# A hybrid decoder layer on one core: position mixes a block earlier, their gelu product on VectorE, and a scan without its empty state

## The chip, the cores and the metric

One core of one Trainium2 chip runs the whole layer in one launch. The metric is device time in microseconds (us). The time before is the median of three runs.

## What is computed

One decoder layer on 1024 tokens of 1024 channels, float32. A normalised input is projected to all inputs of three token mixers; their outputs, each projected and weighted by a sigmoid gate, are summed, projected and added to the residual; a squared-ReLU MLP follows.

```python
def gmlp_mixer(za, ln_g, ln_b, w_s, b_s):              # mixer A
    u, v = jnp.split(jax.nn.gelu(za), 2, axis=-1)
    v = layer_norm(v, ln_g, ln_b)
    vc = v.reshape(bsz, nc, GMLP_CHUNK, GMLP_GROUPS, GMLP_GROUP_DIM)
    w = jnp.where(causal, w_s, 0)                      # 8 groups, 128x128 lower triangle
    mixed = jnp.einsum('gts,bcsgd->bctgd', w, vc) + b_s.T[:, :, None]
    return u * mixed.reshape(bsz, seq, GMLP_WIDTH)

def ssd_mixer(...):                                    # mixer C, 8 chunks of 128 tokens
    ...
    y_diag = jnp.einsum('bgcls,bgrcls,bcsgrp->bclgrp', cb, decay, xdt)
    states = jnp.einsum('bcsgn,bgrcs,bcsgrp->cbgrpn', bc, decay_states, xdt)
    def step(h, inp):
        dec, st = inp
        return h * dec[..., None, None] + st, h        # the state ahead of each chunk
    _, prev = lax.scan(step, jnp.zeros_like(states[0]), (chunk_decay, states))
    y_off = jnp.einsum('bclgn,cbgrpn,bgrcl->bclgrp', cc, prev, jnp.exp(a_cs))
    y = y_diag + y_off + x32 * d_skip
    ...

hn = rms_norm(h, norm_mix_g);  proj = hn @ w_in        # split into za, zb, zc, xbc, dt, gates
merged = sum(sigmoid(gate_k) * (mixer_k @ w_branch_k)) # A gMLP, B recurrence (RG-LRU), C scan (SSD)
h = h + merged @ w_out
h = h + relu(rms_norm(h) @ w_mlp_up)**2 @ w_mlp_down;  out = rms_norm(h)
```

The state ahead of chunk 0 is zero, and the state behind the last chunk (7) is used by nothing.

## The kernel before, in words

Activations lie with channels on the 128 partitions and tokens along the free side. A large float32 product is made from a high part (rounded to float32r) and a low part, three matmuls for each 128x128 weight tile: high by high, high by low, low by high. `split` (L128) makes such a pair: a copy on ScalarE (L132) and a subtraction on VectorE (L133).

The kernel runs in stages:

- Up to about 120 us the normalised input X is built and the V half of gMLP is projected, normalised and written to memory (`vn_d`).
- Then come 34 *units*. A unit (`one_unit`, L567) is a block of 128 output columns of `w_in`: 48 matmuls of 512 columns into a PSUM tile `ps` of two banks (pool `mainps`, two tiles), then its `post` and then `step`, which advances each pending generator by one stage. The units are four groups of the scan (B, C, two X blocks) with two heads of the recurrence each, and then eight U blocks of gMLP (`gmlp_unit`). Weights are loaded and split up to two units ahead (`ahead`); the low part is made by an accumulating DMA on GpSimd's queue (L537).
- Then come the gate blocks in pairs (class `Pair`): each pair is a scheme of seven half-size products (`p1` to `p7`, 12 matmuls each, `seventh`), with sums of weights (`Weights`: `cast1`, `sums1`, `sums2`, `cast12`, `cast34`, `cast22`) and sums of X (`x_forms`: T1 to T4, made for two pairs of k tiles in turn, four stages each). Its PSUM pool `gps` takes the four banks of `mainps` over; pool `aux` has four banks of its own.
- Branch projections, output projection and MLP follow. The change doesn't touch them.

Up to the end of the units the order on each engine is set by the framework's planner: from simulated times it takes, on each engine, the ready instruction that comes first in the program, and a tile is given a buffer when one is free. Generators (`later`, `step`) thus set the program's order, not the exact place. From the gate pairs on (`manual_schedule`) the order is the program's own. Most tiles of 128x1024 share one pool of 15 buffers (tag `act`, names `a`); tiles half as large share 16 (`half`, names `h`).

gMLP before: `post` of U block g makes the gelu of U (`gelu2`, L233 to L238: two steps on ScalarE, two on VectorE), asks for the V group g + 1 (`v_group`, L833) and puts off `stages`. These run one block later: 16 mix matmuls (L847), scale and bias on VectorE (L848), the product with the gelu on GpSimd (L850), and the store (L851). The sums of X and the first pair's weights are put off from the first step of `stages` of blocks 0 and 5.

The scan before: for each of four groups and two halves of the tokens, `rows_in` and `s1_` load decay rows (L666, L672), transpose X and B (L678, L685), weight X (L681, L682) and build the masked matrix; `s2_` makes the states of four chunks (L712) and advances the state (L723, four steps of 64 columns for each chunk); `s3_` adds the state's part (`yo`, L732), the part within the chunk (`yi`, L736) and the skip (L738 to L740), and stores.

Of the kernel before, what the change touches and what calls it, by code (L numbers as in the profile page):

```python
# [36 lines left out]
def trunk_kernel(ctx: ExitStack, tc: tile.TileContext, x, norm_mix_g, w_in, b_gate, gmlp_ln_g, gmlp_ln_b,  # L37
# [40 lines left out]
    def aux():  # L78
        return auxp.tile([P, HF], F32, tag="aux", name=nm("aux"))
# [12 lines left out]
    def hsl(h):  # L92
        return slice(h * HF, h * HF + HF)
# [451 lines left out]
    def later(gen):  # L545
        pending.append(gen)
# [106 lines left out]
    def ssd_stages(g, S):  # L653
        Bf, Cf, Xf = S["b"], S["c"], (S["x0"], S["x1"])
        hs = slice(4 * g, 4 * g + 4)
        Bt = act((P, NCH, P))
        xdt, xw, E, cb, pv, er = {}, {}, {}, {}, {}, {}

        def tok(c):
            return slice(c * P, (c + 1) * P)  # L660

        def rows_in(half):
            for q in (2 * half, 2 * half + 1):
                e = E[q] = act((P, 2, 4, P))
                for cc in range(2):
                    nc.gpsimd.dma_start(out=e[:, cc], in_=acs_v[0, 2 * q + cc, hs, :].partition_broadcast(P))  # L666

        def s1_(half):
            for j in range(2):
                t = er[half, j] = half_((P, 4, P))  # L670
                for h in range(2):
                    nc.gpsimd.dma_start(out=t[64 * h:64 * h + 64], in_=acs_v[1, half * 4:half * 4 + 4, 4 * g + 2 * j + h, :].partition_broadcast(64))  # L672
            for q in (2 * half, 2 * half + 1):
                ps = aux()
                for cc in range(2):
                    for j in range(2):
                        o = cc * 256 + j * P
                        nc.tensor.transpose(out=ps[:, o:o + P], in_=Xf[j][:, tok(2 * q + cc)], identity=ident)  # L678
                ev = ps.rearrange("p (c h d) -> p c h d", c=2, h=4)
                xdt[q], xw[q] = half_((P, 2, 4, 64)), half_((P, 2, 4, 64))  # L680
                tt(out=xdt[q], in0=ev, in1=dt[:, 2 * q:2 * q + 2, hs].unsqueeze(3).to_broadcast([P, 2, 4, 64]), op=ALU.mult)  # L681
                tt(out=xw[q], in0=ev, in1=w2[:, 2 * q:2 * q + 2, hs].unsqueeze(3).to_broadcast([P, 2, 4, 64]), op=ALU.mult)  # L682
            ps = aux()
            for i in range(4):
                nc.tensor.transpose(out=ps[:, tok(i)], in_=Bf[:, tok(half * 4 + i)], identity=ident)  # L685
            actv(Bt[:, half * 4:half * 4 + 4, :], ps.rearrange("p (c n) -> p c n", c=4), AF.Copy)
            cb[half] = aux()
            for i in range(4):
                c = half * 4 + i
                mm(cb[half][:, tok(i)], Bf[:, tok(c)], Cf[:, tok(c)], start=True, stop=True)  # L690

            cbm = half_((P, 4, P))
            tt(out=cbm, in0=cb[half].rearrange("p (c l) -> p c l", c=4), in1=tri.unsqueeze(1).to_broadcast([P, 4, P]), op=ALU.mult)
            for q in (2 * half, 2 * half + 1):
                e = E[q]
                for cc in range(2):
                    for h in range(4):
                        col = (2 * q + cc) * 16 + 4 * g + h
                        actv(e[:, cc, h, :], e[:, cc, h, :], AF.Relu, scale=-1.0, bias=acs[:, col:col + 1])
                actv(e, e, AF.Exp, scale=-1.0)  # L700
                for cc in range(2):
                    i = (2 * q + cc) % 4
                    tt(out=e[:, cc], in0=e[:, cc], in1=cbm[:, i].unsqueeze(1).to_broadcast([P, 4, P]), op=ALU.mult)

        def s2_(half):
            for q in (2 * half, 2 * half + 1):
                if q == 0:
                    pv[0] = half_((P, 2, 256))
                    nc.gpsimd.memset(pv[0][:, 0, :], 0.0)
                st = aux()  # L710
                for cc in range(2):
                    mm(st[:, cc * 256:cc * 256 + 256], Bt[:, 2 * q + cc, :], xw[q][:, cc].rearrange("p h d -> p (h d)"), start=True, stop=True)  # L712
                for cc in range(2):
                    c = 2 * q + cc
                    if c == NCH - 1:
                        continue
                    if cc == 1:
                        pv[q + 1] = half_((P, 2, 256))
                    dst = pv[(c + 1) // 2][:, (c + 1) % 2, :]
                    for h in range(4):  # L720
                        col = c * 16 + 4 * g + h
                        o = slice(h * 64, h * 64 + 64)
                        stt(out=dst[:, o], in0=pv[q][:, cc, o], scalar=etot[:, col:col + 1],  # L723
                            in1=st[:, cc * 256 + h * 64:cc * 256 + h * 64 + 64], op0=ALU.mult, op1=ALU.add)

        def s3_(half):
            tk = hsl(half)
            for j in range(2):
                yo, yi = aux(), aux()
                for i in range(4):  # L730
                    c = half * 4 + i
                    mm(yo[:, tok(i)], pv[c // 2][:, c % 2, j * P:(j + 1) * P], Cf[:, tok(c)], start=True, stop=True)  # L732
                for i in range(4):
                    c = half * 4 + i
                    for h in range(2):
                        mm(yi[64 * h:64 * h + 64, tok(i)], xdt[c // 2][:, c % 2, 2 * j + h, :], E[c // 2][:, c % 2, 2 * j + h, :], start=True, stop=True)  # L736
                y = er[half, j].rearrange("p c l -> p (c l)")
                tt(out=y, in0=yo, in1=y, op=ALU.mult)  # L738
                tt(out=y, in0=yi, in1=y, op=ALU.add)
                stt(out=y, in0=Xf[j][:, tk], scalar=dcol[:, 2 * g + j:2 * g + j + 1], in1=y, op0=ALU.mult, op1=ALU.add)  # L740
                nc.gpsimd.dma_start(out=yr_d[2 * g + j][:, tk], in_=y)

        rows_in(0)
        yield
        if g:
            yield
        s1_(0)
        yield
        s2_(0)
        yield  # L750
        s3_(0)
        rows_in(1)
        yield
        s1_(1)
        yield
        s2_(1)
        yield
        s3_(1)


    PLAIN = 6

    def lru_units(h):
        S = {}

        def post_x(ps):
# [11 lines left out]
                S["xs"].append(p_)  # L778
            if h < PLAIN:
                later(stages(False))  # L780
            elif h == 7:
                v_group(0)

        def post_g(ps):
            S["g2"] = act()
            gelu2(S["g2"], ps, T)
            later(stages(True))

        def stages(gated):
            if not gated:  # L790
# [39 lines left out]
    def v_group(g):  # L830
        if g < 8:
            v_of[g] = act((P, NCH, P))
            nc.gpsimd.dma_start(out=v_of[g], in_=vn_d[:, g * P:(g + 1) * P].rearrange("(c p) d -> p c d", p=P))  # L833

    def gmlp_unit(g):
        def stages(u2):
            if g == 0:
                later(x_forms())
            elif g == 5:
                later(first_pair())  # L840
            yield
            vg = v_of.pop(g)
            y = act()
            for half in range(2):
                ps = aux()
                for i in range(4):
                    mm(ps[:, i * P:(i + 1) * P], vg[:, half * 4 + i, :], wT[:, g, :], start=True, stop=True)  # L847
                stt(out=y[:, hsl(half)].rearrange("p (c t) -> p c t", t=P), in0=ps.rearrange("p (c t) -> p c t", t=P),  # L848
                    scalar=vh[:, LNG + g:LNG + g + 1], in1=bs[:, g, :].unsqueeze(1).to_broadcast([P, 4, P]), op0=ALU.mult, op1=ALU.add)
            nc.gpsimd.tensor_tensor(out=y, in0=y, in1=u2, op=ALU.mult)  # L850
            nc.gpsimd.dma_start(out=yd["a"][g], in_=y)  # L851

        def post(ps):
            u2 = act()
            gelu2(u2, ps, T)
            later(stages(u2))
            v_group(g + 1)

        unit_in(C_U + g * P, post)

# [51 lines left out]
    class Pair:  # L912
# [79 lines left out]
            actv(self.o[0][:, 0], self.b1, AF.Copy)  # L992

        def p2(self):
            b0 = gps.tile([P, HF], F32, tag="gps", name=nm("gps"))
            self.mul(b0, "A12", "B21", True)
            tt(out=self.o[0][:, 0], in0=b0, in1=self.o[0][:, 0], op=ALU.add)

# [916 lines left out]
```

## Time and profile before

| | |
|---|---|
| median of three runs | 1932.02 us (1931.97 to 1932.76) |
| the profiled execution, its own time | 1931.48 us |
| its span in the profile | 1929.8 us |
| TensorE busy | 1896.3 us (98%) |
| VectorE, ScalarE, GpSimd busy | 1408.0, 1010.1, 254.8 us |
| mean granted clock of TensorE | 0.997 |

The profile is of one execution. A row of the timeline has the start, the time from the first start to the last end, the engine, the line of the kernel, the operation and the tiles (out<-in), the shape and a count; behind it in brackets the engine's idle time and what ended it. Successive matmuls overlap: the distance from start to start is what one costs. TensorE (PE) and its weight load (PEld) have rows of their own; DVE is VectorE, ACT ScalarE, POOL GpSimd, SP the queue of SyncE.

### The profile page before, as it was taken

To read this page: it belongs to the slowest core of one execution; us is meant where nothing else is said; L and a number is where in the kernel's file an instruction comes from. 1 tells how busy PE (TensorE), PEld (TensorE's weight loads), DVE (VectorE), ACT (ScalarE), POOL (GpSimd) and SP (SyncE) were. 2 spreads that over 40 slices of the span, in tenths; PEclk is the share of its full clock that TensorE was granted. 3 is DMA by queue.
4 is the path that set the end of the run, shared out by engine and by line. 5 is a ranking of instruction groups with operands and counts; after the bars stand their busy time and mean duration, and the time that the engine had idled before them with its cause. 6 is when DMAs were issued, how large, how long until landed. Compare 5 with 4: busy or idle time off the path is not lost.

```text
span 1929.8 us, 23698 instructions
## 1 busy us (share of the span) xinstructions
PE 1896.3 (98%) x8928; PEld 1582.3 (82%) x8928; DVE 1408.0 (73%) x2005; ACT 1010.1 (52%) x1470; POOL 254.8 (13%) x352
## 2 busy tenths in 40 slices
PE   8999999999999999999999999999999999999998
PEld 7998888888887787878778888887888887888886
DVE  6585869787758776767767889458665567787787
ACT  6435859676634545454554544256655555253236
POOL 4112112121342000000010110000111111000000
PEclk9999999999999999999999999999999999999999
DMA  5346475565755343435298887431554458544532
GB/s 165 79 137 145 112 158 124 123 161 131 162 141 153 109 145 103 156 91 161 93 292 302 229 242 199 159 110 55 180 166 167 137 185 301 184 142 142 176 119 109
DMA packets 210439, 301.25 MB, mean 156 GB/s; under 512 B 12964, under 2 KB 125812, under 8 KB 210324
## 3 DMA queue, kind: packets, MB, share of 16 engines
q1 hardware_dynamic: 166628, 158.28, 26.5%
q0 software_dynamic: 34544, 119.69, 23.1%
q10 hardware_dynamic: 9152, 21.77, 3.2%
q8 instruction: 70, 1.15, 0.2%
q14 instruction: 45, 0.37, 0.1%
HBM read 195.75 MB, written 74.58 MB: 140 GB/s over the span
## 4 chain that ended last, share of the span: by engine, by line
PE 80%; DVE 7%; issue 6%; DMA 3%; ACT 3%; POOL 1%; POOLq 0%; DVEq 0%; ACTq 0%; SPq 0%
PE aux L487 40%; PE ps L564 16%; PE gps L487 10%; PE aux L1387 5%; PE aux L257 4%; PE aux L800 1%; DMA c<-yc_d 1%; PE aux L736 1%; DMA raw<-in_w_in_dram 1%; PE aux L732 1%; DVE wt L133 1%; PE aux L712 1%; DVE a L133 1%; ACT wt L132 1%; DMA a<-g_d 1%
## 5 line engine op out<-in xcount | busy, mean ns | idle before, releaser
L564 PE MATMUL ps<-xn,wh 128*128 128x512 f32 x1088 | 295.1, 392 | 0.0
L487 PE MATMUL aux<-b,b 128*128 128x512 f32 x1152 | 264.4, 390 | 0.7 <-DVE b L133 0.7
L487 PEld LDWEIGHTS aux<-b,b 128*128 128x128 f32 x1152 | 216.1, 188 | 46.7 <-DVE b L133 1.6
L564 PEld LDWEIGHTS ps<-xn,wh 128*128 128x128 f32 x1088 | 202.9, 188 | 42.1 <-issue 0.7
L487 PE MATMUL aux<-a,b 128*128 128x512 f32 x960 | 219.4, 389 | 0.0
L487 PEld LDWEIGHTS aux<-a,b 128*128 128x128 f32 x960 | 180.2, 188 | 37.4
L564 PE MATMUL ps<-xn,wl 128*128 128x512 f32 x544 | 168.4, 390 | 0.0
L487 PE MATMUL gps<-xn,wt 128*128 128x512 f32 x684 | 159.8, 392 | 2.1 <-DVE a L238 2.1
L487 PE MATMUL aux<-b,wt 128*128 128x512 f32 x672 | 156.9, 389 | 0.0
L487 PEld LDWEIGHTS gps<-xn,wt 128*128 128x128 f32 x684 | 128.9, 189 | 29.2 <-issue 2.5
L487 PEld LDWEIGHTS aux<-b,wt 128*128 128x128 f32 x672 | 126.2, 188 | 26.2
L132 ACT ACTIVATE b<-wt 128x1024 fp32r<-128x1024 f32 x88 | 90.7, 1052 | 85.7 <-DMA wt<-u_d 62.0
L133 DVE TENSOR_TENSOR wt<-a,wt 128x1024 fp32r<-128x1024 f32 x66 | 80.8, 1225 | 65.1 <-ACT wt L132 65.0
L564 PEld LDWEIGHTS ps<-xn,wl 128*128 128x128 f32 x544 | 102.1, 188 | 21.4
L133 DVE TENSOR_TENSOR b<-wt,b 128x1024 fp32r<-128x1024 f32 x88 | 107.2, 1219 | 15.4 <-ACT b L132 15.4
L1625 DVE TENSOR_TENSOR a<-aux,a 128x512 f32<-128x512 f32 x112 | 77.1, 688 | 49.3 <-PE aux L487 49.0
L133 DVE TENSOR_TENSOR a<-a,a 128x1024 fp32r<-128x1024 f32 (+1 forms) x68 | 66.5, 985 | 41.8 <-ACT a L132 41.7
L132 ACT ACTIVATE a<-a 128x1024 fp32r<-128x1024 f32 (+1 forms) x68 | 55.7, 833 | 53.2 <-DVE a L1577 45.4
L133 DVE TENSOR_TENSOR wt<-rt,wt 128x1024 fp32r<-128x1024 f32 x35 | 42.8, 1224 | 52.6 <-ACT wt L132 52.5
L487 PE MATMUL aux<-a,wt 128*128 128x512 f32 x336 | 78.7, 390 | 1.2 <-ACT a L1500 1.2
L132 ACT ACTIVATE wt<-a 128x1024 fp32r<-128x1024 f32 x66 | 69.6, 1055 | 12.5 <-DVE a L515 12.1
L487 PEld LDWEIGHTS aux<-a,wt 128*128 128x128 f32 x336 | 62.9, 188 | 15.0 <-ACT a L1500 2.0
(358 smaller groups left out, 3497.9 us busy)
## 6 DMA issues: line engine op xcount, KB each, us to landing
wt<-u_d SPq DMA_DIRECT2D x54, 512.0 KB
u_d<-a POOLq DMA_DIRECT2D x48, 512.0 KB, 4.9
raw<-in_w_in_dram SPq DMA_DIRECT2D x34, 512.0 KB
wl<-raw POOLq DMA_DIRECT2D x34, 512.0 KB, 5.2
g_d<-a POOLq DMA_DIRECT2D x24, 512.0 KB, 3.3
a<-g_d ACTq DMA_DIRECT2D x24, 512.0 KB
rt<-in_w_in_dram SPq DMA_DIRECT2D x19, 512.0 KB
a<-in_w_in_dram SPq DMA_DIRECT2D x19, 512.0 KB
```

The source lines that it names most:

```text
L132: actv(dst_hi, src, AF.Copy)
L133: (eng or nc.vector).tensor_tensor(out=dst_lo, in0=src, in1=dst_hi.bitcast(F32), op=ALU.subtract)
L257: mm(ps[:, :nt], X.tok(a, k, c), wk[k][w], start=(k == 0 and i == 0), stop=(k == KD - 1 and i == 2))
L487: mm(ps, lhs[l][kk], rhs[r][kk], start=(new and n == 0), stop=(n == 11), skip_group_check=not new)
L564: mm(ps[:, hsl(h)], w[wi][:, k, :], a.rhs(ai, k, h), start=(n == 0), stop=(n == 3 * KD - 1))
L712: mm(st[:, cc * 256:cc * 256 + 256], Bt[:, 2 * q + cc, :], xw[q][:, cc].rearrange("p h d -> p (h d)"), start=True, stop=True)
L732: mm(yo[:, tok(i)], pv[c // 2][:, c % 2, j * P:(j + 1) * P], Cf[:, tok(c)], start=True, stop=True)
L736: mm(yi[64 * h:64 * h + 64, tok(i)], xdt[c // 2][:, c % 2, 2 * j + h, :], E[c // 2][:, c % 2, 2 * j + h, :], start=True, stop=True)
L800: mm(ps, w[wi][:, q * P:(q + 1) * P], S["xs"][half][ai], start=(n == 0), stop=(n == 2))
L1387: mm(ps, M.tok(a, k, c), wo[nb][k][w], start=(k == 0 and a + w == 0), stop=(k == KD - 1 and a == 1))
L1625: tt(out=h, in0=ps, in1=h, op=ALU.add)
```

## The change

- **Scan.** The state product of chunk 7, the transpose of its B block and its weighted X (`xw`) are left out, and so are the two products of chunk 0 with the zero state and the rows of decay for it. The state behind chunk 0 is one copy of `st` in place of four multiply-adds with zero, and the zero fill on GpSimd goes. In `s3_`, half 0, the first two steps and the skip run on 384 columns, with a short step for chunk 0.
- **gMLP.** The mix becomes a generator of its own, `mix(g)`, put off in `post` of block g - 1 (for g = 0 in the gate unit of head 7), so that it runs one block ahead of U block g. `post` of block g then makes gelu and, on VectorE, its product with the finished mix, and stores. V groups 0 and 1 are asked for in the X units of heads 6 and 7, group g + 2 in `post` of block g.
- **Sums of X and the first pair's weights** are put off in `post` itself, one block sooner.
- **First pair.** `p2` of the first pair takes its PSUM tile from `aux`, no longer from `gps`.

```diff
@@ ssd_stages
+        def chunks_into(q):
+            return min(2, NCH - 1 - 2 * q)
...
-                    nc.gpsimd.dma_start(out=t[64 * h:64 * h + 64], in_=acs_v[1, half * 4:half * 4 + 4, 4 * g + 2 * j + h, :].partition_broadcast(64))
+                    c0 = 4 * half + (half == 0)
+                    nc.gpsimd.dma_start(out=t[64 * h:64 * h + 64, c0 - 4 * half:], in_=acs_v[1, c0:half * 4 + 4, 4 * g + 2 * j + h, :].partition_broadcast(64))
...
-                tt(out=xw[q], in0=ev, in1=w2[:, 2 * q:2 * q + 2, hs].unsqueeze(3).to_broadcast([P, 2, 4, 64]), op=ALU.mult)
+                n = chunks_into(q)
+                tt(out=xw[q][:, :n], in0=ev[:, :n], in1=w2[:, 2 * q:2 * q + n, hs].unsqueeze(3).to_broadcast([P, n, 4, 64]), op=ALU.mult)
...
-            for i in range(4):
+            nt = 4 - half
+            for i in range(nt):
                 nc.tensor.transpose(out=ps[:, tok(i)], in_=Bf[:, tok(half * 4 + i)], identity=ident)
...
-                    nc.gpsimd.memset(pv[0][:, 0, :], 0.0)
                 st = aux()
-                for cc in range(2):
+                for cc in range(chunks_into(q)):
                     mm(st[:, cc * 256:cc * 256 + 256], Bt[:, 2 * q + cc, :], ...)
...
+                    if c == 0:
+                        nc.vector.tensor_copy(out=dst, in_=st[:, :256])
+                        continue
@@ s3_
+            c0 = P * (half == 0)
...
-                for i in range(4):
+                for i in range(c0 // P, 4):
                     c = half * 4 + i
                     mm(yo[:, tok(i)], pv[c // 2][:, c % 2, j * P:(j + 1) * P], Cf[:, tok(c)], start=True, stop=True)
...
-                tt(out=y, in0=yo, in1=y, op=ALU.mult)
-                tt(out=y, in0=yi, in1=y, op=ALU.add)
-                stt(out=y, in0=Xf[j][:, tk], scalar=dcol[...], in1=y, op0=ALU.mult, op1=ALU.add)
+                tt(out=y[:, c0:], in0=yo[:, c0:], in1=y[:, c0:], op=ALU.mult)
+                tt(out=y[:, c0:], in0=yi[:, c0:], in1=y[:, c0:], op=ALU.add)
+                if c0:
+                    stt(out=y[:, :c0], in0=x_[:, :c0], scalar=d, in1=yi[:, :c0], op0=ALU.mult, op1=ALU.add)
+                stt(out=y[:, c0:], in0=x_[:, c0:], scalar=d, in1=y[:, c0:], op0=ALU.mult, op1=ALU.add)
@@ lru_units
             if h < PLAIN:
                 later(stages(False))
-            elif h == 7:
-                v_group(0)
+            else:
+                v_group(h - PLAIN)
...
             later(stages(True))
+            if h == 7:
+                later(mix(0))
@@ gmlp_unit
+    def mix(g):
+        vg = v_of.pop(g)
+        y = ya[g] = act()
+        for half in range(2):
+            ps = aux()
+            for i in range(4):
+                mm(ps[:, i * P:(i + 1) * P], vg[:, half * 4 + i, :], wT[:, g, :], start=True, stop=True)
+            stt(out=y[...], in0=ps..., scalar=vh[:, LNG + g:LNG + g + 1], in1=bs[:, g, :]..., op0=ALU.mult, op1=ALU.add)
+        yield
+
     def gmlp_unit(g):
-        def stages(u2):
-            ... (sums of X or first pair, yield, the same mix)
-            nc.gpsimd.tensor_tensor(out=y, in0=y, in1=u2, op=ALU.mult)
-            nc.gpsimd.dma_start(out=yd["a"][g], in_=y)
         def post(ps):
-            u2 = act()
+            u2, y = act(), ya.pop(g)
             gelu2(u2, ps, T)
-            later(stages(u2))
-            v_group(g + 1)
+            tt(out=y, in0=y, in1=u2, op=ALU.mult)
+            nc.gpsimd.dma_start(out=yd["a"][g], in_=y)
+            if g + 1 < 8:
+                later(mix(g + 1))
+            v_group(g + 2)
+            if g == 0:
+                later(x_forms())
+            elif g == 5:
+                later(first_pair())
@@ Pair
         def p2(self):
-            b0 = gps.tile([P, HF], F32, tag="gps", name=nm("gps"))
+            b0 = gps.tile([P, HF], F32, tag="gps", name=nm("gps")) if prev else aux()
```

More of the change, by code (lines that the diff above doesn't have):

```diff
@@ L681, in s1_ @@
                 tt(out=xdt[q], in0=ev, in1=dt[:, 2 * q:2 * q + 2, hs].unsqueeze(3).to_broadcast([P, 2, 4, 64]), op=ALU.mult)
-                tt(out=xw[q], in0=ev, in1=w2[:, 2 * q:2 * q + 2, hs].unsqueeze(3).to_broadcast([P, 2, 4, 64]), op=ALU.mult)
+                n = chunks_into(q)
+                tt(out=xw[q][:, :n], in0=ev[:, :n], in1=w2[:, 2 * q:2 * q + n, hs].unsqueeze(3).to_broadcast([P, n, 4, 64]), op=ALU.mult)
             ps = aux()
-            for i in range(4):
+            nt = 4 - half
+            for i in range(nt):
                 nc.tensor.transpose(out=ps[:, tok(i)], in_=Bf[:, tok(half * 4 + i)], identity=ident)
-            actv(Bt[:, half * 4:half * 4 + 4, :], ps.rearrange("p (c n) -> p c n", c=4), AF.Copy)
+            actv(Bt[:, half * 4:half * 4 + nt, :], ps[:, :nt * P].rearrange("p (c n) -> p c n", c=nt), AF.Copy)
             cb[half] = aux()
@@ L708, in s2_ @@
                     pv[0] = half_((P, 2, 256))
-                    nc.gpsimd.memset(pv[0][:, 0, :], 0.0)
                 st = aux()
-                for cc in range(2):
+                for cc in range(chunks_into(q)):
                     mm(st[:, cc * 256:cc * 256 + 256], Bt[:, 2 * q + cc, :], xw[q][:, cc].rearrange("p h d -> p (h d)"), start=True, stop=True)
-                for cc in range(2):
+                for cc in range(chunks_into(q)):
                     c = 2 * q + cc
-                    if c == NCH - 1:
-                        continue
                     if cc == 1:
@@ L726, in s3_ @@
         def s3_(half):
-            tk = hsl(half)
+            c0 = P * (half == 0)
             for j in range(2):
                 yo, yi = aux(), aux()
-                for i in range(4):
+                for i in range(c0 // P, 4):
                     c = half * 4 + i
@@ L736, in s3_ @@
                         mm(yi[64 * h:64 * h + 64, tok(i)], xdt[c // 2][:, c % 2, 2 * j + h, :], E[c // 2][:, c % 2, 2 * j + h, :], start=True, stop=True)
-                y = er[half, j].rearrange("p c l -> p (c l)")
-                tt(out=y, in0=yo, in1=y, op=ALU.mult)
-                tt(out=y, in0=yi, in1=y, op=ALU.add)
-                stt(out=y, in0=Xf[j][:, tk], scalar=dcol[:, 2 * g + j:2 * g + j + 1], in1=y, op0=ALU.mult, op1=ALU.add)
-                nc.gpsimd.dma_start(out=yr_d[2 * g + j][:, tk], in_=y)
+                y, x_ = er[half, j].rearrange("p c l -> p (c l)"), Xf[j][:, hsl(half)]
+                d = dcol[:, 2 * g + j:2 * g + j + 1]
+                tt(out=y[:, c0:], in0=yo[:, c0:], in1=y[:, c0:], op=ALU.mult)
[3 more added lines that the diff above has]
+                stt(out=y[:, c0:], in0=x_[:, c0:], scalar=d, in1=y[:, c0:], op0=ALU.mult, op1=ALU.add)
+                nc.gpsimd.dma_start(out=yr_d[2 * g + j][:, hsl(half)], in_=y)
         rows_in(0)
@@ L833, in v_group, with post @@
             nc.gpsimd.dma_start(out=v_of[g], in_=vn_d[:, g * P:(g + 1) * P].rearrange("(c p) d -> p c d", p=P))
-    def gmlp_unit(g):
-        def stages(u2):
+    ya = {}
+    def mix(g):
[5 more added lines that the diff above has]
+                mm(ps[:, i * P:(i + 1) * P], vg[:, half * 4 + i, :], wT[:, g, :], start=True, stop=True)
+            stt(out=y[:, hsl(half)].rearrange("p (c t) -> p c t", t=P), in0=ps.rearrange("p (c t) -> p c t", t=P),
+                scalar=vh[:, LNG + g:LNG + g + 1], in1=bs[:, g, :].unsqueeze(1).to_broadcast([P, 4, P]), op0=ALU.mult, op1=ALU.add)
+        yield
+    def gmlp_unit(g):
+        def post(ps):
+            u2, y = act(), ya.pop(g)
+            gelu2(u2, ps, T)
+            tt(out=y, in0=y, in1=u2, op=ALU.mult)
[3 more added lines that the diff above has]
+            v_group(g + 2)
             if g == 0:
@@ L840, in stages @@
                 later(first_pair())
[L841 to L850, printed above, removed]
-            nc.gpsimd.dma_start(out=yd["a"][g], in_=y)
-        def post(ps):
-            u2 = act()
-            gelu2(u2, ps, T)
-            later(stages(u2))
-            v_group(g + 1)
         unit_in(C_U + g * P, post)
```

## The prediction

> **What bounds the kernel now.** I read the page's first part, then the busy time by stretch, then TensorE's instructions in order of time around the one stretch that stood out.
>
> ```profile
> PE 1896.3 (98%) x8928; PEld 1582.3 (82%) x8928; DVE 1408.0 (73%) x2005; ACT 1010.1 (52%) x1470; POOL 254.8 (13%) x352
> ...
> 120.00:320.00 200.00, 198.84 (x997) 165.65 (x996) 153.43 (x259) 134.28 (x191) 38.92 (x61) 1.00 0.58 131
> 320.00:490.00 170.00, 169.93 (x909) 142.54 (x909) 130.93 (x204) 121.12 (x188) 38.37 (x61) 1.00 0.63 142
> 490.00:583.00 93.00, 93.00 (x500) 79.33 (x499) 62.15 (x77) 40.35 (x56) 36.26 (x26) 1.00 0.60 155
> 583.00:640.00 57.00, 52.80 (x239) 42.69 (x238) 46.47 (x50) 23.08 (x32) 13.33 (x8) 0.97 0.42 130
> ```
>
> The columns of a stretch are its length, then busy time of TensorE, its weight load, VectorE, ScalarE and GpSimd, then granted clock, DMA share and GB/s. TensorE is busy for 1896.3 of 1929.8 us. From 120 to 583 us, where the scan, the recurrence and the position mixes run, it idles 1.2 us in all: there the time is the sum of TensorE's instructions, and any instruction taken out shortens it, while work taken off VectorE or GpSimd is worth nothing by itself. The change ends at about 615 us, and the one bad place within its reach is the passage from the last U block to the first gate pair, just after 590 us:
>
> ```profile
> 590.61 3.73 PE L847 MATMUL aux<-wT,a 128*128 128x128 f32 x32
> 594.10 2.98 PE L487 MATMUL gps<-xn,wt 128*128 128x512 f32 x12
> 599.17 4.17 PE L487 MATMUL gps<-xn,wt 128*128 128x512 f32 x12 [2.10 <-DVE a L238]
> 603.14 1.06 PE L487 MATMUL aux<-h,wt 128*128 128x512 f32 x2
> 605.08 2.59 PE L487 MATMUL aux<-h,wt 128*128 128x512 f32 x10 [0.88 <-DVE wt L133]
> 607.97 3.04 PE L487 MATMUL gps<-h,wt 128*128 128x512 f32 x12 [0.30 <-ACT a L992]
> ...
> 612.37 2.56 PE L487 MATMUL aux<-xn,wt 128*128 128x512 f32 x10 [0.92 <-DVE wt L133]
> 614.77 8.32 PE L487 MATMUL gps<-xn,wt 128*128 128x512 f32 x36
> ...
> 625.65 2.88 PE L487 MATMUL aux<-h,wt 128*128 128x512 f32 x12
> 628.37 2.88 PE L487 MATMUL gps<-h,wt 128*128 128x512 f32 x12
> ```
>
> These are p1, p2, p5, p6, p3 of the first pair, 12 matmuls each. From 594.10 to 614.77 they take 20.67 us. At the steady spacing (628.37 - 625.65 = 2.72 us for 12) they need 13.60. So 7.07 us are lost here. Four waits (2.10, 0.88, 0.30, 0.92) make 4.20 of it. The clock makes another part:
>
> ```profile
> 599.17:602.00 2.83, 2.83 (x10) 2.30 (x11) 2.83 (x5) 1.13 (x2) 0.00 (x0) 0.77 0.60 164
> 602.00:605.00 3.00, 2.20 (x6) 1.20 (x4) 3.00 (x5) 0.44 (x1) 2.15 (x1) 0.65 0.62 169
> 605.00:608.00 3.00, 2.62 (x11) 1.84 (x11) 3.00 (x4) 0.69 (x2) 2.70 (x2) 1.00 0.09 26
> ```
>
> Right behind the 2.10 us wait the granted clock is 0.77 and 0.65: 0.23 x 2.83 + 0.35 x 3.00 = 1.70 us. The other 1.17 us is the filling and emptying of the pipeline at each stop.
>
> **The change, part by part.**
>
> *Scan without unneeded state.* Per group it drops one transpose of B (L685), one state product (L712) and two products with a zero state (L732, chunk 0, one for each j). There are four groups.
>
> ```profile
> L685 PE MATMUL aux<-ident,a x32: 272/273/273, 175.5 to 496.6; 128*128 128x128 f32 x32
> L712 PE MATMUL aux<-h,a x64: 376/379/380, 187.8 to 510.1; 128*128 128x256 f32 x64
> L732 PE MATMUL aux<-a,h x128: 269/275/378, 203.2 to 525.8; 128*128 128x128 f32 x128
> 450.00 0.60 PE L685 MATMUL aux<-ident,a 128*128 128x128 f32 x4
> 450.43 1.06 PE L690 MATMUL aux<-a,a 128*128 128x128 f32 x8
> 477.58 1.05 PE L732 MATMUL aux<-a,h 128*128 128x128 f32 x8
> 478.56 1.09 PE L736 MATMUL aux<-a,h 128*64 128x128 f32 x16
> 508.54 1.89 PE L712 MATMUL aux<-h,a 128*128 128x256 f32 x8
> 510.27 1.95 PE L847 MATMUL aux<-wT,a 128*128 128x128 f32 x16
> 511.97 1.17 PE L564 MATMUL ps<-xn,wh 128*128 128x512 f32 x4
> ```
>
> 32 transposes for 4 x 8 chunks are one instruction each; 64 for 32 state products and 128 for 64 products with the state are two each. The price of one is the distance from start to start, not its own length, since they overlap. Transpose: 0.43 / 4 = 0.108 us, 4 of them, 0.43. State product: 8 instructions in 1.73 us (508.54 to 510.27), 0.216 each, and 8 go: 1.73. Product with the state: 0.98 / 8 = 0.123 us, or 0.106 as the 128-column ones of the mix take (1.70 / 16), and 16 go: 1.70 to 1.96. Sum 3.9 to 4.1; I take 4.0, all of it on the path because TensorE does not wait there. The rest of this part is VectorE work (half of one L682 product, four L723 steps for one copy, L738 to L740 on 384 columns, with one more short step for chunk 0), four GpSimd memsets, and smaller row loads. None is on the path: the cover is TensorE's unbroken row of unit products, with weights two units ahead. Without that cover one extra VectorE step would cost what it takes, below 0.7 us.
>
> *Product with gelu on VectorE.*
>
> ```profile
> 529.44 1.22 DVE L886 TENSOR_TENSOR a<-xn,a 128x1024 f32<-128x1024 f32 x1
> 587.53 2.89 DVE L133 TENSOR_TENSOR h<-a,h 128x512 fp32r<-128x512 f32 x1
> 603.81 1.22 DVE L133 TENSOR_TENSOR wt<-a,wt 128x1024 fp32r<-128x1024 f32 x1
> 604.94 1.40 DVE L848 SCALAR_TENSOR_TENSOR a<-aux,vh,bs 128x512 f32<-128x512 f32 x2
> 606.26 2.10 DVE L133 TENSOR_TENSOR xn<-a,xn 128x1024 fp32r<-128x1024 f32 x1
> 608.29 2.89 DVE L133 TENSOR_TENSOR a<-a,a 128x512 fp32r<-128x512 f32 x1
> 611.11 1.21 DVE L133 TENSOR_TENSOR wt<-a,wt 128x1024 fp32r<-128x1024 f32 x1
> 586.63 3.24 POOL L850 TENSOR_TENSOR a<-a,a 128x1024 f32<-128x1024 f32 x1 [6.18 <-DVE a L848]
> 608.18 2.45 POOL L850 TENSOR_TENSOR a<-a,a 128x1024 f32<-128x1024 f32 x1
> ```
>
> Eight products of about 1.22 us (as L886) join VectorE, 9.8 us, and eight slower ones (3.24 and 2.45 us here) leave GpSimd. While GpSimd runs one, VectorE is held: the half-size splits at 587.53 and 608.29 take 2.89 us, where a full one takes 1.22, and end just behind GpSimd's product. So VectorE pays 9.8 us and gets part of it back. From 490 to 583 us it is busy 62 of 93 us, so the price there is nothing.
>
> *Mix one block ahead.* The 16 mix matmuls of each block stay (8 x 1.70 us), but all eight now stand ahead of the end of the last U block: the 32 at 590.61 move forward, and the first pair's p1 follows that block at once. Against p1 this is neutral: as many matmuls as before lie ahead of it. Behind the last U block are left its gelu and one product.
>
> *p2 in another bank.* The first b0 comes from aux, so the wait for L238 (2.10) and the clock's 1.70 behind it go. What is late next? p5 needs cast12's low part (ends 603.81 + 1.22 = 605.03 now), and would be due at 594.10 + 2 x 2.72 = 599.54; p3 needs cast34's (611.11 + 1.21 = 612.32), due at 594.10 + 4 x 2.72 = 604.98. Both sit in VectorE's queue, which is busy all through the stretches shown above (2.83 of 2.83, then 3.00 of 3.00 twice). Of that queue, ahead of cast12, the sums of X of one stage (L886, L887 and two half-size splits, some 2 x 1.1 + 2 x 0.6 = 3.4 us, and the 2.2 that the split at 587.53 was held) move a block earlier, four L848 move ahead (two take 1.3, so 2.6), and two products come (2.3): 5.9 us sooner, 599.1. Ahead of cast34 also the two holds by GpSimd at 606 to 611 go (2.10 - 1.22 = 0.9, and 2.2), and L848 at 604.94 is counted already: 603.3. Both come out just in time, by 0.4 and 1.7 us. The four waits then cost between 0 and, if nothing in VectorE's queue moves, the full 7.07. The middle of such narrow margins is a wait of about 1 us; I take 6.0 us back, near the end at which all goes, since the queue's own sum says so.
>
> The Trainium skill ("TensorE: Matmul & The Clock Gate", Part 1, the table of two states) says that the clock halves after at least one idle window of about 3.4 us. By that rule the 2.10 us wait alone would not have lowered it, and the sum would be 4.0 + 4.3 = 8.3 us. The rows above show 0.77 and 0.65 behind 2.10 us of idling, so I go by the rows.
>
> *One block sooner, loads included.* A V group is asked for at the end of block g for use at the end of block g + 1, where it had two blocks.
>
> ```profile
> 512.07 1.22 POOL L833 DMA_DIRECT2D a<-vn_d  x1
> DMA to landing us min/median/max: 5.6/7.2/7.8
> ```
>
> The second U block ends at 508.54 (the L712 row above starts there), the load is issued 3.5 us later, behind the accumulating weight load in GpSimd's queue, and lands 5.6 to 7.8 us after that: at most 11.3 us. A block is 48 matmuls, 4 x 2.72 = 10.9 us, and 1.70 for its mix: 12.6. The cover is thus 1.3 us at the worst, and I cost it at nothing.
>
> **Sum.** 4.0 + 6.0 = 10.0 us. The profiled execution took 1931.48 us (span 1929.8, 1.7 around it), 0.5 below the median of 1932.02. From the median: 1922.0 us.
>
> **The rivals.**
>
> *The wait moves to p5 (B).* Only L238's wait goes, and VectorE delivers cast12 and T1 late, because the 15 shared buffers (tag act), for which the sums of X must wait, are all taken, and asking a block sooner changes nothing. For it: VectorE's queue is full in the rows above, and margins of 0.4 and 1.7 us are thin. Against it: gelu's buffer now goes free behind a product of 1.22 us on VectorE, no longer behind a later mix and GpSimd. If p5 waits 4 us, the passage gives 2 and the time is 1932.0 - 4.0 - 2 = 1926.0. If nothing is gained there, 1928.0.
>
> *V groups come late (C), the other side.* The mix of block g + 1 waits for its load between two units. It decides once the issue slips by over 1.3 us. If six blocks wait 2 us each, 12 us are lost, and with the clock's 1.70 behind each 10 more: 1934 to 1944. Against it: the queue that held L833 loses the GpSimd products; and a wait under 1 us left the clock at 1.00 (605 to 608).
>
> *The clock's drop is not tied to the wait (D).* It has another cause and comes anyway: the gain is 10.0 - 1.7 = 8.3, 1923.7. Against it: nothing else in the stretch idles TensorE before the drop. The idle window of the Trainium skill's page named above would give the same time.
>
> *All of the passage is returned (A+).* Nothing waits: 4.1 + 7.1 = 11.2, 1920.8.
>
> **How the numbers follow.** The forecast with A+ beside it 0.58 (1920.8 to 1923), D 0.09, B 0.22 (1924 to 1929), C 0.06, something I do not see, with either sign, 0.05. The predicted time is 1922.0. The likeliest case's own range is 1920 to 1924. The 8-in-10 range drops the upper end of B and C, and at the lower end only what lies 1.5 us beyond A+: 1919 to 1928.5. About 0.2%, 3.9 us, is what a measurement of this kernel can tell from no change, so faster means below 1928.2. That holds in the forecast, in D, in most of B (0.16) and in part of the unseen: 0.85. Same takes the rest of B and a little of C: 0.09. Slower 0.06.
>
> **What would show it.** In the profile after: 28 L685, 56 L712 and 112 L732 instructions; no 32 mix matmuls behind the last unit; p1 directly behind it and p2 without a wait; the clock at 1.00 through the passage; five products of the first pair in 13.6 to 15 us; no GpSimd tensor operation, and no VectorE split of 2 to 3 us. TensorE's busy time falls by about 5.7 us (4.0 and the clock's 1.7), its idle time by about 4. The prediction is wrong if p5 or p6 waits over 2 us, if TensorE waits for a V group's load between units, or if TensorE idles more than 1.2 us between 120 and 583.

## The result, and the profile after

| | before | after |
|---|---|---|
| median, eleven runs each | 1932.03 us | 1927.88 us |
| after over before, 95% interval | | 0.9975 (0.9967 to 0.9984) |
| span of the profiled execution | 1929.8 us | 1926.2 us |
| start to the first unit (first L564) | 119.54 | 122.48 |
| the units (to the first pair's p1) | 474.56 | 474.94 |
| passage (p1 to p7) | 20.67 | 13.60 |
| the rest | 1315.03 | 1315.18 |

The change is faster by 4.1 us, where 10.0 were forecast. The last four lines are differences of starts in the two traces. The passage gave 7.07 us, all that was lost in it. The units gave nothing at all, though work of TensorE was taken out of them, and the start came out 2.9 us longer, though nothing in it was changed. The passage after, in TensorE's instructions in order of time:

```profile
597.42 2.88 PE L487 MATMUL gps<-xn,wt 128*128 128x512 f32 x12
600.14 2.88 PE L487 MATMUL aux<-xn,wt 128*128 128x512 f32 x12
602.86 2.88 PE L487 MATMUL aux<-h,wt 128*128 128x512 f32 x12
605.58 2.88 PE L487 MATMUL gps<-h,wt 128*128 128x512 f32 x12
608.30 2.88 PE L487 MATMUL aux<-xn,wt 128*128 128x512 f32 x12
611.02 5.15 PE L487 MATMUL gps<-xn,wt 128*128 128x512 f32 x22
```

Five products at 2.72 us, no bracket, so no idle time. Now the busy time by stretch, with the columns of the prediction's table:

```profile
PE 1892.8 (98%) x8900; PEld 1579.0 (82%) x8900; DVE 1405.4 (73%) x2009; ACT 1003.8 (52%) x1466; POOL 222.1 (12%) x340
...
120.00:320.00 200.00, 198.44 (x995) 165.22 (x994) 152.46 (x262) 128.97 (x187) 37.73 (x58) 1.00 0.55 127
320.00:490.00 170.00, 168.37 (x902) 140.79 (x901) 129.53 (x204) 119.18 (x185) 38.56 (x60) 1.00 0.65 147
490.00:583.00 93.00, 91.90 (x493) 78.14 (x493) 69.91 (x89) 39.52 (x56) 16.37 (x23) 1.00 0.65 164
583.00:640.00 57.00, 57.00 (x261) 47.51 (x260) 43.16 (x50) 25.86 (x33) 2.52 (x4) 1.00 0.37 112
```

The last stretch is full, and its clock is 1.00. The first three idle 1.56, 1.63 and 1.10 us: 4.3 in all, where it was 1.2. The waits of TensorE between 120 and 583 us name them, first before, then after (the tile and line that waited, for what, total, times, longest):

```profile
PE aux L800 <- ACT a L686: 1.2, 1, 1.2
```

```profile
PE aux L811 <- DVE h L687: 1.4, 1, 1.4
PE aux L811 <- ACT a L692: 1.3, 1, 1.3
PE aux L854 <- ACT a L692: 1.1, 1, 1.1
PE aux L811 <- DVE h L729: 0.2, 1, 0.2
PE aux L696 <- DVE h L746: 0.2, 1, 0.2
```

L811 is the recurrence's product (L800 before), L854 the mix, L692 the copy of transposed B (L686 before). The wait of 1.3 is the old one; the four others, 2.9 us, are new. The one of 1.4 is near 450 us, and the chain that ends there can be read backwards (start, us, what):

```profile
432.99 11.38 DMA raw<-in_w_in_dram
...
444.39 1.06 ACT wh L535
...
446.70 1.76 ACT a L705 x6
...
449.45 0.62 ACT h L132
...
450.09 0.04 DVE h L133
...
453.25 0.61 DVE h L687
...
453.99 0.93 PE aux L811 x3
```

Before, the same stretch (440 to 456 us) has no engine but TensorE on its chain. After, TensorE stands at L811 because VectorE has not emptied the PSUM tile (L687). VectorE is late because L133 ahead of it waits for ScalarE's split of the recurrence's input (L132). ScalarE is late because it waited for a weight tile: L535 copies the raw tile, whose load went out at 432.99. Where that comes from shows in ScalarE's, GpSimd's and SP's rows, before:

```profile
408.00 1.06 ACT L535 ACTIVATE wh<-raw 128x1024 fp32r<-128x1024 f32 x1 [0.33 <-PE ps L564]
410.75 2.46 ACT L699 ACTIVATE a<-a,acs 128x128 f32<-128x128 f32 x8
...
420.22 0.88 POOL L537 DMA_DIRECT2D wl<-raw  x1 [10.98 <-ACT wl L536]
...
425.44 5.02 SPq L532 DMA_DIRECT2D raw<-in_w_in_dram  x2
...
436.22 1.04 ACT L535 ACTIVATE wh<-raw 128x1024 fp32r<-128x1024 f32 x1
...
443.34 1.15 ACT L132 ACTIVATE h<-a 128x512 fp32r<-128x512 f32 x2 [0.89 <-DVE a L587]
```

and after:

```profile
414.69 2.51 ACT L705 ACTIVATE a<-a,acs 128x128 f32<-128x128 f32 x8 [2.68 <-DMA a<-acs_d]
...
421.84 1.04 ACT L535 ACTIVATE wh<-raw 128x1024 fp32r<-128x1024 f32 x1
...
426.18 0.88 POOL L537 DMA_DIRECT2D wl<-raw  x1 [16.26 <-ACT wh L535]
...
432.99 2.31 SPq L532 DMA_DIRECT2D raw<-in_w_in_dram  x2
...
444.39 1.06 ACT L535 ACTIVATE wh<-raw 128x1024 fp32r<-128x1024 f32 x1 [2.76 <-DMA raw<-in_w_in_dram]
...
449.45 1.13 ACT L132 ACTIVATE h<-a 128x512 fp32r<-128x512 f32 x2
```

One weight tile's copy stood ahead of the decay steps (L699) at 408.00. After, the planner puts it behind them (L705), and they wait 2.68 us for their rows from memory: 421.84. There are two raw tiles. One is refilled when its low part, too, has been made from it (L537, at 420.22 before and 426.18 after), so the load goes out at 432.99, where it was 425.44. The whole profile after starts 2.9 us later; counted from the first unit, the load slips by 4.6 us. The copy of that tile waits 2.76 us. What stands behind that copy on ScalarE, and behind the split on VectorE, is late too: L132 by 6.1 us (443.34, 449.45), 3.2 counted from the first unit. Neither engine goes past a waiting instruction in these rows. The Trainium skill ("PSUM — Partial Sum Buffer", Engine vs sequencer instructions) calls their queues strict FIFO; the rows agree.

### The profile page after: what moved, and what is told of

The parts are those of the page before. It is cut to its first block, busy times and chain, and to the rows that moved or that the text cites. A ratio compares the mean times of both kernels' runs of the same rounds, so it can differ in the third digit from the quotient of the medians.

```text
span 1926.2 us, 23611 instructions
## 1 busy us (share of the span) xinstructions
PE 1892.8 (98%) x8900; PEld 1579.0 (82%) x8900; DVE 1405.4 (73%) x2009; ACT 1003.8 (52%) x1466; POOL 222.1 (12%) x340
## 4 chain that ended last, share of the span: by engine, by line
PE 78%; DVE 7%; DMA 5%; ACT 5%; issue 5%; POOL 1%; SPq 0%; POOLq 0%; ACTq 0%; DVEq 0%
PE aux L487 41%; PE ps L564 13%; PE gps L487 11%; PE aux L1401 5%; PE aux L257 4%; DMA raw<-in_w_in_dram 2%; PE aux L811 1%; DMA a<-acs_d 1%; ACT wt L132 1%; DVE wt L133 1%; PE aux L854 1%; DVE a L587 1%; DMA wl<-raw 1%; PE aux L1661 1%; DVE a L133 1%
## 5 line engine op out<-in xcount | busy, mean ns | idle before, releaser
L564 PE MATMUL ps<-xn,wh 128*128 128x512 f32 x1088 | 296.2, 392 | 0.0
L564 PEld LDWEIGHTS ps<-xn,wh 128*128 128x128 f32 x1088 | 202.8, 188 | 42.3 <-issue 1.0
L564 PE MATMUL ps<-xn,wl 128*128 128x512 f32 x544 | 167.6, 389 | 0.0
L487 PE MATMUL gps<-xn,wt 128*128 128x512 f32 x672 | 155.6, 389 | 0.0
L132 ACT ACTIVATE b<-wt 128x1024 fp32r<-128x1024 f32 x88 | 90.7, 1053 | 86.3 <-DMA wt<-u_d 50.3
L133 DVE TENSOR_TENSOR wt<-a,wt 128x1024 fp32r<-128x1024 f32 x66 | 80.8, 1225 | 66.5 <-ACT wt L132 66.4
L564 PEld LDWEIGHTS ps<-xn,wl 128*128 128x128 f32 x544 | 102.1, 188 | 21.6
L133 DVE TENSOR_TENSOR b<-wt,b 128x1024 fp32r<-128x1024 f32 x88 | 107.1, 1218 | 17.1 <-ACT b L132 17.1
L133 DVE TENSOR_TENSOR a<-a,a 128x1024 fp32r<-128x1024 f32 (+1 forms) x68 | 64.3, 953 | 41.4 <-ACT a L132 41.3
L132 ACT ACTIVATE a<-a 128x1024 fp32r<-128x1024 f32 (+1 forms) x68 | 55.7, 834 | 52.8 <-DVE a L1591 45.2
L133 DVE TENSOR_TENSOR wt<-rt,wt 128x1024 fp32r<-128x1024 f32 x35 | 42.9, 1224 | 49.5 <-ACT wt L132 49.4
L132 ACT ACTIVATE wt<-a 128x1024 fp32r<-128x1024 f32 x66 | 69.6, 1055 | 10.9 <-DVE a L515 10.5
```

Source lines behind the costliest of these rows:

```text
L132: actv(dst_hi, src, AF.Copy)
L133: (eng or nc.vector).tensor_tensor(out=dst_lo, in0=src, in1=dst_hi.bitcast(F32), op=ALU.subtract)
L487: mm(ps, lhs[l][kk], rhs[r][kk], start=(new and n == 0), stop=(n == 11), skip_group_check=not new)
L564: mm(ps[:, hsl(h)], w[wi][:, k, :], a.rhs(ai, k, h), start=(n == 0), stop=(n == 3 * KD - 1))
```

## Experiments

Ratios are to the kernel before on the same chip (its median was 1932.03 us beside the change, 1933.08 for the next four runs, 1933.63 for the four behind them and 1933.52 for the last two), with 95% intervals. "Idle" is TensorE's in the stretch 320 to 490 us; "copy" says whether the weight copy (L535) in question stands ahead of the decay steps on ScalarE or behind them; "tile asked" is when the load that refills its raw tile goes out, counted from the first unit.

| run | units | passage | idle | copy | tile asked | median us | ratio |
|---|---|---|---|---|---|---|---|
| before | 474.56 | 20.67 | 0.07 | ahead | 305.9 | 1932.02 | |
| the change | 474.94 | 13.60 | 1.63 | behind | 310.5 | 1927.88 | 0.9975 (0.9967 to 0.9984) |
| scan alone | 472.80 | 20.65 | 0.65 | behind | 310.8 | 1930.09 | 0.9985 (0.9977 to 0.9994) |
| all but the scan | 476.49 | 13.60 | 0.07 | ahead | 307.5 | 1927.36 | 0.9973 (0.9962 to 0.9983) |
| p2's bank alone | 475.32 | 20.91 | 0.07 | ahead | 306.9 | 1933.6 | 1.0001 (0.9992 to 1.0009) |
| all but p2's bank | 475.55 | 17.54 | 1.71 | behind | 310.8 | 1930.19 | 0.9987 (0.9978 to 0.9996) |
| change, zero fill kept | 473.80 | 13.60 | 0.07 | ahead | 305.6 | 1924.26 | 0.9954 (0.9941 to 0.9966) |
| the same, mix first | 474.50 | 13.60 | 0.78 | ahead | 306.8 | 1924.88 | 0.9955 (0.9941 to 0.9968) |
| the change again | 479.05 | 13.60 | 2.65 | behind | 312.3 | 1928.78 | 0.9975 (0.9966 to 0.9984) |
| product on GpSimd | 475.86 | 15.04 | 2.07 | behind | 310.7 | 1928.31 | 0.9977 (0.9968 to 0.9987) |
| change, full decay rows | 473.32 | 13.60 | 0.27 | ahead | 302.3 | 1924.54 | 0.9955 (0.9941 to 0.9968) |
| zero fill kept, again | 473.54 | 13.60 | 0.07 | ahead | 306.2 | 1923.93 | 0.9951 (0.9938 to 0.9963) |

In all five profiles with the copy behind, the recurrence's product waits 0.6 to 1.4 us for VectorE near 450 us. Of the seven with the copy ahead, five have no such wait; the other two (0.7 with the mix first, 0.20 with the full rows) wait at the end of a chain that starts at a load of decay rows (12.1 and 8.6 us long), not of weights.

### The scan's part alone

The kernel before with the edits of `ssd_stages` and `s3_` alone:

```diff
-                for cc in range(2):
+                for cc in range(chunks_into(q)):
                     mm(st[:, cc * 256:cc * 256 + 256], Bt[:, 2 * q + cc, :], ...)
...
-                    nc.gpsimd.memset(pv[0][:, 0, :], 0.0)
...
-                for i in range(4):
+                for i in range(c0 // P, 4):
                     c = half * 4 + i
                     mm(yo[:, tok(i)], ...)
```

> The kernel before with the scan part alone. From the first unit product to p1 of the first pair the kernel before takes 474.56 us. The scan part takes 4.0 us of TensorE's work out. Theory (the planner's new order on ScalarE, made by the scan part, casts a weight tile later, its raw buffer is refilled later, and TensorE waits for the scan and recurrence banks near 450 us): 474.56 - 4.0 + 2.0 = 472.6 us there, with TensorE waits of over 1 us on VectorE steps of the scan; passage from p1 to p7 unchanged at 20.7; in all 2 us faster than before. Rival (the V group loads in GpSimd's queue made that delay): no such wait, 470.6 us, 4 us faster.

The units became 1.76 us shorter. Compared by the start of the same instruction in both traces, each group starts its next piece 0.43, 0.11 and 0.42 us earlier where products with the state, transpose and state product are gone: 3.9 us over the four groups, as forecast. The other 2.1 us were given back: 0.9 near 450 us, where the tile is asked for 4.9 us later than before and L809 waits 0.58 us (over 1 was expected), 0.4 in the first group, and 0.8 in the second, where L809 waits 1.9 us for the copy of transposed B (1.2 before). So the loss near 450 belongs to the scan's part: without that part (next run) that stretch idles 0.07 us, as before.

### All but the scan

The change with `ssd_stages` as before:

```diff
-            for i in range(nt):
+            for i in range(4):
                 nc.tensor.transpose(out=ps[:, tok(i)], in_=Bf[:, tok(half * 4 + i)], identity=ident)
...
-                for cc in range(chunks_into(q)):
+                for cc in range(2):
```

> The change without its scan part: mixes ahead, product on VectorE, sums sooner, p2 in aux. Theory: no wait near 450 us; the second mix still waits 1.1 us for a bank behind the last group's transposes (1.3 us in all); first unit to p1 474.56 + 1.3 = 475.9 us; passage from p1 to p7 13.6 us; 5.8 us faster than before. Rival (V group loads delay the weights): the waits near 450 us are there too, 477.9 us, 3.8 us faster.

The passage is all back, and the units are 1.93 us longer than before though no work was added to TensorE in them. By the starts of the same instructions, 1.1 us of that falls around the second mix, which waits for a bank (see the mix put first), and 0.8 on the first two groups, where the bank alone, in the next run, also lost 0.8 before any of its edit came into play. The ratio, 0.9973, cannot be told from that of the whole change, 0.9975: as it stands there, the scan's part adds nothing that these runs can tell.

### p2's bank alone, and all but p2's bank

The first is the kernel before with this one line, the second the change without it:

```diff
-            b0 = gps.tile([P, HF], F32, tag="gps", name=nm("gps"))
+            b0 = gps.tile([P, HF], F32, tag="gps", name=nm("gps")) if prev else aux()
```

> The kernel before with p2's bank alone changed. Theory: the wait moves to p5, whose cast12 part ends at the same time as before (605.0 us), so the passage from p1 to p7 stays near 20.7 us, and the time within 0.7 us of before. Rival: the wait for L238 and the clock's drop were the loss, 3.8 us faster.

> The whole change with p2 back in its old bank. Theory: p2 waits for the last gelu step, 2.1 us, and the clock drops behind it, 1.7 us: passage from p1 to p7 17.4 us against 13.6, time 3.8 us above that of the change. Rival (the sums of X sooner give all, and the wait hides): under 1 us above.

TensorE's rows of the first pair, the bank alone:

```profile
596.13 2.98 PE L487 MATMUL gps<-xn,wt 128*128 128x512 f32 x12
603.59 5.43 PE L487 MATMUL aux<-xn,wt 128*128 128x512 f32 x12 [4.48 <-DVE a L848]
```

and all but the bank:

```profile
601.31 4.57 PE L487 MATMUL gps<-xn,wt 128*128 128x512 f32 x12 [2.10 <-DVE a L238]
605.71 2.88 PE L487 MATMUL aux<-h,wt 128*128 128x512 f32 x12
```

The bank alone takes the wait away from L238 and finds one twice as long behind the mix (L848), which holds the aux banks: the passage is 20.91 us, 0.24 longer. The length was as expected, but it is p2 that waits, not p5. Without the bank the 2.10 us wait stays, and the twelve matmuls behind it take 605.71 - 601.31 = 4.40 us for 2.72, at a granted clock of 0.61: a drop worth 1.7 us. The other waits are gone. By the ratios this version is 2.3 us slower than the change, where 3.8 were expected. So the passage needs both the bank and the rest of the gMLP part; neither gives 7 us. Of that rest only the product was tried by itself (below); the mix and the sums were not.

### The zero fill kept, and again

The change, but the state ahead of chunk 0 is filled with zeros on GpSimd and advanced by four multiply-adds, as before. TensorE's work is that of the change.

```diff
+                    nc.gpsimd.memset(pv[0][:, 0, :], 0.0)
...
-                    if c == 0:
-                        nc.vector.tensor_copy(out=dst, in_=st[:, :256])
-                        continue
```

> The whole change, but the zero fill of the first state on GpSimd and its four multiply-adds in each group are kept (VectorE and GpSimd work alone; TensorE's work is that of the change). With it the planner puts the weight casts on ScalarE where the kernel before has them. Theory (the change lost its gain to that order): first unit to p1 474.56 - 3.9 (scan) + 1.3 (second mix waits for a bank) + up to 0.8 of scatter = 472.0 to 472.8 us against the change's 474.9, no TensorE wait near 450 us over 0.5 us; passage 13.6; 9 us faster than before. Rival (the waits come from bank use or V loads, whatever the order of the casts): 474.9 us, 6.7 us faster.

> The change with the zero fill and the four multiply-adds kept, the same text as the earlier run of that name, for the same chip as the full decay rows. Theory (a stable gain from the order): again no wait over 0.5 us near 450, units 473 to 474.5, passage 13.6, 0.9945 to 0.9965 of before. Rival (the good run was chance of clock and start, not of the order): units 475 or more, ratio above 0.9965.

More work on GpSimd and VectorE made the kernel faster than the change. The weight tile is asked for 305.6 and 306.2 us behind the first unit (305.9 before), and the stretch 320 to 490 idles 0.07 us, as before. The interval of the first run (0.9941 to 0.9966) ends where those of the change begin (0.9967 and 0.9966), that of the second (to 0.9963) lies clear of them. The first run's units missed what was expected by 1.0 us: the second mix's wait is 1.4 us here, and the first group waits 0.7.

### The mix put first

The version with the zero fill, and the mix ahead of the other pending generators:

```diff
-                later(mix(g + 1))
+                pending.insert(0, mix(g + 1))
```

> As the kernel with the zero fill kept, and the pending mix is put ahead of the scan's stage in each step, so that the second mix stands before the last group's transposes on TensorE. Theory (the mix waited for banks that the transposes held): the 1.3 us go, first unit to p1 470.7 to 471.5 us, 10 to 11 us faster than before. Rival (the transposes then wait for the mix's banks, as VectorE is full there): same as with the mix behind, or slower by 1 us.

The wait of the second mix goes, and the next instruction has it:

```profile
502.99 0.52 PE L691 MATMUL aux<-ident,a 128*128 128x128 f32 x3 [0.89 <-DVE h L687]
```

The units are 474.50 us, where 470.7 to 471.5 were expected; the rival came. The mix's place in the list only decides which of them stands. In the change itself it was the mix:

```profile
502.93 1.16 PE L854 MATMUL aux<-wT,a 128*128 128x128 f32 x8 [1.10 <-ACT a L692]
```

There are four aux banks; the last group's X, B, masked matrix and the mix want them at once, and ScalarE's copy (L692) must free one.

### The change again

Unedited, for the scatter of start and units.

> The change itself once more, for its start. The profile of the change reached the first unit 2.9 us later than the profile of before (122.5 against 119.5 us), with the same instructions in the same order. Theory (chance: where the clock's drops fall): a start between 119.5 and 121.5 us here, first unit to p1 474.9 within 0.8. Rival (the change makes the start longer): 122.5 us again.

The start is 119.27 us, 3.2 shorter than in the first profile of the same program. The units were expected within 0.8 us of the first profile's; they are 4.1 longer, with the same chain, the tile asked for 312.3 us behind the first unit, and these two waits near 450:

```profile
450.65 1.16 PE L696 MATMUL aux<-a,a 128*128 128x128 f32 x8 [0.70 <-DVE h L746]
453.20 1.62 PE L811 MATMUL aux<-h,lw 128*128 128x512 f32 x3 [1.39 <-DVE h L687]
```

By the starts ahead of and behind them they cost 4.1 us, where it was 2.1 in the first profile of the change. Most of the difference is the clock: from 452 to 456 us 0.64 is granted here, 1.00 there. The other 2 us of the longer units fell in the groups ahead of this place. The 2.9 us at the start were chance, and are no part of the change. The loss near 450 us is; its size varies.

### The product left on GpSimd

The change with this line as before:

```diff
-            tt(out=y, in0=y, in1=u2, op=ALU.mult)
+            nc.gpsimd.tensor_tensor(out=y, in0=y, in1=u2, op=ALU.mult)
```

> The whole change with the product left on GpSimd. Theory (VectorE's queue had 1.7 to 3 us to spare in the passage, and each product on GpSimd holds VectorE by up to 2.3 us): passage 14 to 16 us against 13.6, time 0.5 to 2.5 us above that of the change. Rival (no matter): 13.6 us and the same time.

VectorE's, GpSimd's and TensorE's rows:

```profile
605.43 4.04 DVE L133 TENSOR_TENSOR a<-a,a 128x1024 fp32r<-128x1024 f32 x2
...
605.60 3.32 POOL L863 TENSOR_TENSOR a<-a,a 128x1024 f32<-128x1024 f32 x1 [9.76 <-DVE a L238]
...
609.39 1.21 DVE L133 TENSOR_TENSOR wt<-a,wt 128x1024 fp32r<-128x1024 f32 x1
...
610.66 2.58 PE L487 MATMUL aux<-xn,wt 128*128 128x512 f32 x10 [0.91 <-DVE wt L133]
```

While GpSimd runs its product, two splits on VectorE take 4.04 us; in the change the same two take 1.22 and 0.69. cast34's low part behind them ends at 610.60, p3 waits 0.91 for it, and the passage is 15.04. The product's move is worth 1.4 us in the profile; the medians of the two kernels, 1928.31 and 1928.78, do not tell them apart (0.5 to 2.5 us were expected). The Trainium skill ("SBUF — State Buffer", SBUF: two separate sides) says that contention between engines is only at the port that GpSimd and VectorE share; the two rows at 605 agree.

### Full decay rows

If the order on ScalarE loses the time, another edit that leaves the order as before must keep the gain, with no zero fill. The change with the decay rows of all four chunks loaded:

```diff
-                    c0 = 4 * half + (half == 0)
-                    nc.gpsimd.dma_start(out=t[64 * h:64 * h + 64, c0 - 4 * half:], in_=acs_v[1, c0:half * 4 + 4, ...].partition_broadcast(64))
+                    nc.gpsimd.dma_start(out=t[64 * h:64 * h + 64], in_=acs_v[1, half * 4:half * 4 + 4, ...].partition_broadcast(64))
```

> The whole change, but the decay rows of the state's part are loaded for all four chunks of a half, chunk 0's too, as before; no zero fill, one copy for the state behind chunk 0, as in the change. TensorE's work is that of the change. Theory (it is the order in which ScalarE takes weight copies and decay steps that loses the time near 450 us, and any edit that leaves that order as before keeps the gain): the raw weight tile is asked for at 425 to 427 us, no wait over 0.5 us of the recurrence's product (L811) near 450, units 473 to 475, passage 13.6, about 1924 to 1925, ratio 0.9950 to 0.9962. Rival (the time comes from the work that the zero fill and the four multiply-adds put on GpSimd and VectorE, so only keeping those helps): as the change, tile asked for at 431 or later, a wait of 2 us or more near 450, units 475 to 479, ratio 0.9970 to 0.9980.

As the order's theory had it: units 473.32, 0.9955. The same engines' rows as above:

```profile
406.11 1.06 ACT L535 ACTIVATE wh<-raw 128x1024 fp32r<-128x1024 f32 x1 [0.31 <-PE ps L564]
413.07 1.28 ACT L704 ACTIVATE a<-a,acs 128x128 f32<-128x128 f32 x4 [3.34 <-DMA a<-acs_d]
...
421.56 11.28 SPq L532 DMA_DIRECT2D raw<-in_w_in_dram  x2
...
439.63 1.04 ACT L535 ACTIVATE wh<-raw 128x1024 fp32r<-128x1024 f32 x1
...
444.71 1.15 ACT L132 ACTIVATE h<-a 128x512 fp32r<-128x512 f32 x2
...
449.28 0.94 PE L810 MATMUL aux<-h,lw 128*128 128x512 f32 x3 [0.20 <-DVE h L686]
```

The copy at 406.11 is ahead of the decay steps again, the load goes out in time (at 421.56, where 425 to 427 was expected), and L132 is at 444.71. The rival, that the zero fill itself is what helps, falls by the units and the idle time; the interval of the ratio (to 0.9968) just touches that of the change. Yet TensorE still waits 0.20 us here, at the end of the chain from the decay rows: with 3.9 us less of its own work TensorE has come level with it, and the cover that was there before is used up.

## Why the prediction was wrong

**The passage: right, a little too low.** The wait for L238 and the clock's drop went with the bank, as the prediction said. What it feared next was in time: cast12's low part ends at 597.54, 5.3 us ahead of p5's start (forecast 0.4), cast34's at 606.26, 2.0 ahead of p3's (forecast 1.7).

```profile
596.32 1.22 DVE L133 TENSOR_TENSOR wt<-a,wt 128x1024 fp32r<-128x1024 f32 x1
...
605.04 1.22 DVE L133 TENSOR_TENSOR wt<-a,wt 128x1024 fp32r<-128x1024 f32 x1
```

I took 6.0 us and 7.07 came back. Why cast12's part came 4.9 us earlier than the queue's sum said was not taken apart. Rival B did not occur in the change; with the bank alone the wait did move, but to p2 behind the mix. Rival D fell: wherever the waits went, the clock in the passage was 1.00. But the tie to the 2.10 us wait is looser than the prediction had it. In all but the bank the drop came behind that wait; in the scan alone the wait passed without one (twelve matmuls in 2.82 us), and the drop came at the next, longer wait (granted clock 0.72 from 602 to 606 us):

```profile
598.12 2.98 PE L487 MATMUL gps<-xn,wt 128*128 128x512 f32 x12 [2.10 <-DVE a L238]
...
604.02 4.01 PE L487 MATMUL aux<-h,wt 128*128 128x512 f32 x10 [2.37 <-DVE wt L133]
```

The Trainium skill's rule of an idle window of about 3.4 us ("TensorE: Matmul & The Clock Gate", Part 1) would have kept the clock up behind 2.10 us of idling; the 4.40 us for twelve matmuls in all but the bank do not agree.

**The scan's work: right. Its cover: the step that failed.** 3.9 us of TensorE's work went, between the bounds. The failing sentence is "None is on the path: the cover is TensorE's unbroken row of unit products, with weights two units ahead". It costed the smaller engines' edits at nothing because TensorE had unit products to do meanwhile, and took the lead of the weights as given. But edits there change the order in which the planner places everything else, and with less of TensorE's work the same chains have less time. A weight copy fell behind decay steps that wait for memory, the load behind it slipped by 4.6 us against the units, and 2.1 us (4.1 in the other profile) came back as a wait of TensorE, with the clock's drop behind it in the other. The share of idle time on ScalarE did not show this; the chain of in-order instructions from a load to TensorE's next bank does.

**The mix one block ahead: half right.** Neutral against p1, as said. But it was never asked what the second mix now stands beside: the last group's transposes, with four banks for all. It waits 1.10 us, and costs some 1.4 with the stop.

**Product and V groups: right.** No wait for `vn_d` occurs, so rival C did not. The held splits are gone, and VectorE's 69.91 of 93 us from 490 to 583 cost nothing.

**The sum.** In the two profiles: units +0.4 instead of -4.0, passage -7.1 instead of -6.0, start +2.9 by chance, rest +0.15: -3.6 of the span, -4.1 of the medians. In the units, 2.1 near 450, 1.4 at the mix and 0.6 in the first groups make 4.1, against 3.9 saved: 0.2 longer, where 0.4 were measured. Passage and units together give 6.7 us in the first profile of the change and 2.6 in the second; the medians, 4.1 and 4.9, lie between. The prediction named TensorE idling over 1.2 us between 120 and 583 as a sign against it; 4.3 came.

**Open.** Of 11.0 us (3.9 and 7.07) the best versions, with the zero fill or the full decay rows, keep 8.7 to 9.5 by their ratios; the second mix takes most of the rest, and the first two groups' extra waits, 0.2 to 2 us, scatter from run to run, in the bank alone too. Why the load at 432.99 takes 11.4 us was not tried. A third raw tile would test the chain from another side; it was not run.

## What to carry to other kernels

When a planner sets the order, an edit that only takes work away from idle engines is not free: after it, look for the loads whose issue slipped, and follow them along the in-order queues to the bounding engine. When the bounding engine gets shorter by x, every chain that runs beside it from memory has x less time, so a cover must be read as a distance in microseconds, not as a share of busy time. A wait at a hand-over goes only when all that is late next is made early as well; here the bank alone gave nothing, and the reorder without it 3 us of the 7.

## What was not expected of the hardware

The same program with the same wait ran with and without a drop of the clock. Before and after, TensorE waits 2.03 us at 38 us for the same GpSimd step; the stretch behind it, before:

```profile
38.00:42.00 4.00, 3.72 (x26) 3.73 (x27) 1.86 (x7) 3.03 (x10) 4.00 (x5) 1.00 0.00 0
```

and after:

```profile
38.00:42.00 4.00, 3.84 (x19) 3.84 (x20) 1.97 (x7) 3.15 (x10) 4.00 (x5) 0.65 0.00 0
```

The granted clock is 1.00 in one and 0.65 in the other (1.00 again in the second profile of the change). So a wait near 2 us lowers the clock in some executions, not in all. With other drops of this kind the start took between 119.3 and 122.5 us in these profiles, nearly as much as the whole scan's part was to bring: one profile's total does not tell such gains, only its stretches do.
